# Differential attention beside a delta rule: second probabilities scaled by VectorE, diagonal blocks of inverses loaded to their places

## The chip, the core and the metric

The kernel runs on one core of one Trainium2 chip. The metric is the device time of one launch in microseconds (us). The engines are TensorE (PE, and PEld for its weight loads), VectorE (DVE), ScalarE (ACT), GpSimd (POOL), and SyncE (SP), whose queue issues the transfers here.

## The reference, cut to what matters

Two transformer blocks follow each other. The change lies in the mixer of the first, which has two halves that run at the same time: differential attention (four heads) and a gated delta rule (GDN; two directions, ten tiles of 128 tokens, four heads).

```python
def diff_attn(q, k, v, lam):          # 8 query blocks of 128, 4 heads, 1280 keys
    s = einsum('bqhid,bkhid->bhiqk', qi, k)
    p = softmax(s, axis=-1)
    a = p[:, :, 0] - lam * p[:, :, 1]
    return einsum('bhqk,bkhe->bqhe', a, v)
...
def gdn_chunked(q, k, v, g, beta, s0, need_out):
    a_mat = eye + bc * (kc @ kc.T) * dec_strict       # unit lower triangular
    sol = triangular_solve(a_mat, [bc * exp(Gc) * kc, bc * vc])
    def step(s, xs):
        u = ub_n - w_n @ s
        o = qd_n @ s + aqk_n @ u
        return gl_n * s + kd_n.T @ u, o
```

## The kernel before

`stage_mixer` first projects and prepares (`gdn_prep` writes the triangular matrices of every tile to `Ad` in DRAM; `gdn_invert` inverts the four 32x32 diagonal blocks of each matrix on VectorE and writes the inverses and their transposes to `XT` in DRAM). Then comes the stretch in which both halves run side by side; it is called the mixing stage below.

- **Attention.** A unit (`da_unit`) is one block of 128 queries of one head; there are 32. Per softmax `i` (two of them) and per piece of 512, 512 and 256 keys: two matmuls make a score piece `sc` in PSUM (three such buffers), VectorE reduces its minimum (L707, tile `dst`), ScalarE takes the exponential into `E` (L708), which frees the PSUM buffer. Six tiny VectorE operations (L712 to L719) give a factor per row and piece. Then the second probabilities are scaled by GpSimd (L722: three `tensor_mul` per unit, in place on `E[1]`), and VectorE joins both (L723, `scalar_tensor_tensor`). Ten transposes on TensorE (L729), copies by ScalarE (L730), ten products with the values, and a norm whose power is taken by GpSimd (L93) end the unit.
- **Head switch.** `da_load` loads queries, keys and values of a head and splits them into a high and a low part: queries' low parts on VectorE (L674, tile `da_ql`), keys' low parts (L677, tile `da_ka`) on VectorE for head 0 and on GpSimd for heads 1 to 3, two operations per head.
- **Delta rule.** `gdn_merge` builds the whole 128x128 inverse of a tile pair (one tile per direction) from the diagonal blocks: it loads the blocks into `mc` (L489, one transfer per direction, 128 partitions), copies them by sixteen VectorE copies of 32x4x32 into the block diagonals of `X` (L496, tile `mX`, two buffers per direction) and `T` (L497, tile `mT`, one buffer per direction), and fills the off-diagonal blocks by small matmuls. `gdn_step` then uses `X` (first product of the step, `ga<-sv,mX`) and updates the state.
- **What sets the order.** The program emits one delta step per four units from the fourth step on (`DAU`, `DA0`); a scheduler then lays out every engine's instructions, so each engine runs a fixed order, and SP's queue too: a transfer that waits for its buffer holds all that stand behind it.

```python
    for d, t in enumerate(ts):
        c = wk.tile([128, 8, 32], F32, name=f"mc{d}", bufs=2)
        nc.sync.dma_start(c, K.XT[d, t].rearrange("x h b j i -> (b j) (x h) i"))
```

Of the kernel before, what the change touches and what calls it, by code (L numbers as in the profile page):

```python
# [10 lines left out]
F32 = mybir.dt.float32  # L11
# [5 lines left out]
ALU = mybir.AluOpType  # L17
# [452 lines left out]
def gdn_merge(K, wk, ts, first):  # L470
# [3 lines left out]
    nc = K.nc  # L474

    def new(name, n=128, bufs=2):
        return wk.tile([128, 4, n], F32, name=name, bufs=bufs)

    def bank():
        return K.ga.tile([128, 4, 128], F32, name="gm", bufs=GMB)  # L480

    B = [new(f"mB{d}", bufs=1) for d in range(2)]
    X, T = [K.X[d][len(K.done) % 2] for d in range(2)], K.T
    K.done.append(ts)
    k = [new(f"mk{d}") for d in range(2)]
    Xc, Tc = [], []
    for d, t in enumerate(ts):
        c = wk.tile([128, 8, 32], F32, name=f"mc{d}", bufs=2)
        nc.sync.dma_start(c, K.XT[d, t].rearrange("x h b j i -> (b j) (x h) i"))  # L489
        Xc.append(c[:, 0:4])  # L490
        Tc.append(c[:, 4:8])
        nc.sync.dma_start(B[d], K.Ad[d, t].rearrange("h j i -> j h i"))
        nc.sync.dma_start(k[d], K.ktk[t])
        for b in range(4):
            q = slice(b * 32, (b + 1) * 32)
            nc.vector.tensor_copy(X[d][q, :, q], Xc[d][q])  # L496
            nc.vector.tensor_copy(T[d][q, :, q], Tc[d][q])  # L497
    G = new("mG", 64)
    pg = bank()
    pairs = []  # L500
# [3 lines left out]
            pairs.append((d, lo, hi) if d == 0 else (d, hi, lo))  # L504
    for d, F, S in pairs:
        for h in range(4):
            K.mm(pg[S, h, 0:32], B[d][F, h, S], Tc[d][F, h], True, True)
    nc.scalar.activation(G[:, :, 0:32], pg[:, :, 0:32], AF.Copy, scale=-1.0)
    px = bank()
    for d, F, S in pairs:  # L510
        for h in range(4):
            K.mm(px[F, h, 0:32], G[S, h, 0:32], Xc[d][S, h], True, True)
    for d, F, S in pairs:
        nc.scalar.activation(X[d][F, :, S], px[F, :, 0:32], AF.Copy)
    py = bank()
    for d, F, S in pairs:
        for h in range(4):
            K.mm(py[S, h, 0:32], Xc[d][S, h], G[S, h, 0:32], True, True)
    for d, F, S in pairs:
        nc.vector.tensor_copy(T[d][S, :, F], py[S, :, 0:32])  # L520
    pg = bank()
# [136 lines left out]
def da_load(K, hd, lp, h):  # L658
    nc = K.nc
    q = lp.tile([128, L], F32, name="dalq")  # L660
# [4 lines left out]
    nc.sync.dma_start(v, K.vd[:, h * 128:(h + 1) * 128].rearrange("(t p) e -> p t e", p=128))  # L665
    lo, hi = slice(0, 64), slice(64, 128)
    Q, KA = [], []
    sub = (nc.gpsimd if h else nc.vector).tensor_sub
    for i, (a, b) in enumerate(((lo, hi), (hi, lo))):
        qh = hd.tile([128, L], F32R, name=f"da_qh{i}")  # L670
        ql = hd.tile([128, L], F32R, name=f"da_ql{i}")
# [18 lines left out]
def da_unit(K, wk, ek, ps, hd, qb, o):  # L690


    nc = K.nc
# [4 lines left out]
    mn, ls, sc, l2 = (st[:, i] for i in range(4))  # L698
    t = wk.tile([128, 4, 2], F32, name="dsu")
# [87 lines left out]
def stage_mixer(K, cst, dr):  # L787

    nc, I, tc = K.nc, K.I, K.tc
# [21 lines left out]
    with ExitStack() as s0:  # L811
# [4 lines left out]
        with ExitStack() as s1:  # L816
# [6 lines left out]
            with ExitStack() as s2:  # L823
                wk = K.pool(s2, "cvw", 2)
# [30 lines left out]
            wk = dp  # L855
# [14 lines left out]
        with ExitStack() as s1:  # L870
# [40 lines left out]
            n, u = 0, da()  # L911
# [1607 lines left out]
```

## Time and profile before

| | |
|---|---|
| median of three runs | 3204.37 us (3204.27 to 3206.47) |
| the profiled execution's own time | 3200.96 us |
| its span (first to last instruction) | 3199.2 us |
| share of the span busy: PE / DVE / ACT / POOL | 91% / 75% / 51% / 21% |
| mixing stage in the span | about 545 to 1015 us |

The profiled execution ran 3.4 us below the median; its span leaves out 1.8 us around the first and last instruction. The busy shares are averages over stages of different limits, so the mixing stage is read by itself below. PE's busy time is the union of the times of matmuls that overlap; it is an upper bound of the work.

### The profile page before, as it was taken

Reading aid. Unit: us, or ns where it says so; the run is one execution under the profiler, and the core shown is the slowest. Engines: PE = TensorE matmul, PEld = TensorE weight load, DVE = VectorE, ACT = ScalarE, POOL = GpSimd, SP = SyncE. Lnnn points to the kernel's source line nnn. Section 1 sums busy time; section 2 is a strip of 40 time slices with the busy share of each in tenths; the row PEclk is TensorE's granted clock in tenths of the full one; section 3 lists DMA queues with packets and bytes.
Section 4 is the critical chain, followed back from the end, with each engine's and each line's share of the span. In section 5 each row is a group of like instructions: output and inputs, shape, how many; then the busy total and the mean of one; then the engine's idle time right before and its main releaser. Section 6 shows DMA issues by size and latency. Waiting matters only on the chain.

```text
span 3199.2 us, 45340 instructions
## 1 busy us (share of the span) xinstructions
PE 2898.8 (91%) x15797; PEld 2389.5 (75%) x15797; DVE 2396.0 (75%) x4935; ACT 1634.3 (51%) x3127; POOL 661.9 (21%) x606
## 2 busy tenths in 40 slices
PE   6899998779898969999998799998798999999999
PEld 3677886768786748888776677777677788888787
DVE  4388676897887599999988599986556686555675
ACT  3333454464675238877776577654443243333343
POOL 1000111244555511112001334432125000000000
PEclk8999998789899979999999899999899999999999
DMA  6366565443325469999996223224565323333833
GB/s 219 109 212 194 178 189 185 128 140 111 89 89 181 146 227 379 393 393 375 374 372 222 69 66 93 69 71 129 156 220 192 111 77 107 110 109 99 293 112 102
DMA packets 366211, 567.04 MB, mean 177 GB/s; under 512 B 72581, under 2 KB 207646, under 8 KB 365982
## 3 DMA queue, kind: packets, MB, share of 16 engines
q1 hardware_dynamic: 361374, 547.37, 50.5%
q0 software_dynamic: 4608, 16.78, 2.1%
q8 instruction: 124, 2.03, 0.3%
q14 instruction: 105, 0.86, 0.1%
HBM read 446.12 MB, written 117.95 MB: 176 GB/s over the span
## 4 chain that ended last, share of the span: by engine, by line
PE 65%; DVE 18%; DMA 7%; issue 4%; ACT 3%; POOL 2%; SPq 1%; DVEq 0%; ACTq 0%; POOLq 0%
PE pj L57 38%; PE py L57 5%; PE pu L57 5%; PE pg L57 5%; PE ga L57 2%; PE lg L57 2%; DVE dst L707 2%; DMA s5wo<-s5o 1%; DVE E L723 1%; DVE bjv L1778 1%; DMA wmod<-in_w_mod_dram 1%; PE sc L57 1%; PE tp L1252 1%; PE gm L57 1%; DVE tw L1101 1%
## 5 line engine op out<-in xcount | busy, mean ns | idle before, releaser
L1229 DVE TENSOR_TENSOR wl<-wraw,wh 128x1024 fp32r<-128x1024 f32 x384 | 446.6, 1219 | 10.7 <-ACT wh L1228 10.4
L1228 ACT ACTIVATE wh<-wraw 128x1024 fp32r<-128x1024 f32 x384 | 391.8, 1060 | 77.7 <-PE pu L57 39.7
L57 PE MATMUL pj<-hh,wh 128*128 128x512 f32 (+1 forms) x768 | 297.7, 388 | 14.4 <-ACT uo L1928 9.5
L57 PE MATMUL pj<-hl,wh 128*128 128x512 f32 (+1 forms) x768 | 293.3, 382 | 0.0
L57 PE MATMUL pj<-hh,wl 128*128 128x512 f32 (+1 forms) x768 | 292.4, 382 | 0.0
L57 PEld LDWEIGHTS pj<-hh,wh 128*128 128x128 f32 x768 | 146.1, 190 | 46.5 <-ACT uo L1928 12.6
L57 PE MATMUL pj<-wh,hh 128*128 128x512 f32 (+1 forms) x400 | 160.8, 403 | 16.9 <-DVE g L2018 9.0
L57 PEld LDWEIGHTS pj<-hh,wl 128*128 128x128 f32 x768 | 145.4, 190 | 30.4 <-issue 3.7
L57 PEld LDWEIGHTS pj<-hl,wh 128*128 128x128 f32 x768 | 145.8, 190 | 27.1 <-issue 2.9
L708 ACT ACTIVATE E<-sc,dst 128x512 f32<-128x512 f32 (+1 forms) x192 | 117.4, 616 | 94.4 <-DVE dst L707 84.1
L57 PE MATMUL pj<-wh,hl 128*128 128x512 f32 (+1 forms) x400 | 158.9, 399 | 1.7 <-DVE hl L214 1.5
L57 PE MATMUL pj<-wl,hh 128*128 128x512 f32 (+1 forms) x400 | 160.2, 401 | 0.0
L75 ACT ACTIVATE wh<-wraw 128x1024 fp32r<-128x1024 f32 (+2 forms) x88 | 88.7, 1014 | 91.9 <-DMA wraw<-in_w_in_dram 37.3
L76 POOL TENSOR_TENSOR wl<-wraw,wh 128x1024 fp32r<-128x1024 f32 (+1 forms) x44 | 100.7, 2293 | 140.2 <-ACT wh L75 139.9
L57 PE MATMUL sc<-da_ka,da_qh 128*128 128x512 f32 (+1 forms) x192 | 83.6, 438 | 35.7 <-ACT E L708 32.0
L1292 POOL DMA_INDIRECT xacc<-ye,ix x16 | 49.9, 3121 | 318.7 <-DVE ye L1291 238.0
L707 DVE TENSOR_REDUCE dst<-sc 128x1 f32<-128x512 f32 (+1 forms) x192 | 108.6, 593 | 8.2 <-PE sc L57 7.2
L57 PE MATMUL pu<-wl,xh 128*128 128x512 f32 x256 | 101.3, 396 | 9.4 <-DVE wl L1229 9.2
L722 POOL TENSOR_TENSOR E<-E,dst 128x512 f32<-128x512 f32 (+1 forms) x96 | 95.7, 1024 | 55.8 <-DVE dst L719 27.2
L1775 ACT ACTIVATE bja<-isc,bca 128x384 bf16<-128x384 f32 (+2 forms) x96 | 79.4, 827 | 51.3 <-DVE bca L1793 25.4
L57 PEld LDWEIGHTS pj<-wh,hh 128*128 128x128 f32 x400 | 77.7, 195 | 34.8 <-DVE g L2018 9.4
L57 PE MATMUL pg<-wl,xh 128*128 128x512 f32 x256 | 102.8, 402 | 0.5 <-DVE wl L1229 0.5
(825 smaller groups left out, 8508.8 us busy)
## 6 DMA issues: line engine op xcount, KB each, us to landing
wraw<-in_w_gate_dram SPq DMA_DIRECT2D x64, 1024.0 KB
wraw<-in_w_up_dram SPq DMA_DIRECT2D x64, 1024.0 KB
wraw<-in_w_down_dram SPq DMA_DIRECT2D x64, 1024.0 KB
wraw<-in_w_in_dram SPq DMA_DIRECT2D x52, 512.0 KB
raw<-hsd SPq DMA_DIRECT2D x38, 512.0 KB
mw<-in_w_mod_dram SPq DMA_DIRECT2D x32, 512.0 KB
raw<-in_w_ffn_gate_dram SPq DMA_DIRECT2D x22, 512.0 KB
raw<-in_w_ffn_up_dram SPq DMA_DIRECT2D x22, 512.0 KB
```

The costliest lines, as they stand in the source:

```text
L57: self.nc.tensor.matmul(out, lhsT, rhs, start=start, stop=stop, skip_group_check=True)
L75: nc.scalar.activation(h, raw, AF.Copy)
L76: self.sub(l, raw, h.bitcast(F32))
L707: nc.vector.tensor_reduce(mn[:, i, j:j + 1], p[:, :n], axis=AX.X, op=ALU.min)
L708: nc.scalar.activation(e[:, c0:c0 + n], p[:, :n], AF.Exp, bias=mn[:, i, j:j + 1], scale=-1.0, accum_out=ls[:, i, j:j + 1])
L722: nc.gpsimd.tensor_mul(e1, e1, sc[:, 1, j:j + 1].to_broadcast([128, n]))
L723: nc.vector.scalar_tensor_tensor(e0, e0, sc[:, 0, j:j + 1], e1, op0=ALU.mult, op1=ALU.add)
L1101: self.V.tensor_tensor(b[:, :, i], a[:, :, 0], a[:, :, 1], op=ops[i])
L1228: nc.scalar.activation(h, raw[:, k], AF.Copy)
L1229: nc.vector.tensor_sub(l, raw[:, k], h.bitcast(F32))
L1292: nc.gpsimd.indirect_dma_start(out=K.xacc, out_offset=bass.IndirectOffsetOnAxis(ap=idx[e][:, :1], axis=0), in_=ye, in_offset=None, compute ...
L1775: self.K.nc.scalar.activation(jk[:, :self.n], self.x, AF.Sign, bias=cand, scale=-1.0, accum_out=cnt)
```

## The change

1. The second probabilities are scaled on VectorE (`tensor_scalar` with one scalar per partition) and no longer on GpSimd (`tensor_mul` with a broadcast factor).
2. The keys' low parts of heads 1 to 3 are subtracted on VectorE too.
3. `gdn_merge` loads each diagonal block straight to its place: eight transfers of 32 partitions x 4 x 32 elements (16 KB) per direction, four for `X` and four for `T`, take the place of one transfer of 128 KB and eight copies. The tile `mc` is gone; `T` gets a second buffer per direction, cleared once like the others. The small matmuls read the blocks out of `X` and `T`.

```diff
-    X, T = [K.X[d][len(K.done) % 2] for d in range(2)], K.T
+    X, T = ([Y[d][len(K.done) % 2] for d in range(2)] for Y in (K.X, K.T))
...
     for d, t in enumerate(ts):
-        c = wk.tile([128, 8, 32], F32, name=f"mc{d}", bufs=2)
-        nc.sync.dma_start(c, K.XT[d, t].rearrange("x h b j i -> (b j) (x h) i"))
-        Xc.append(c[:, 0:4])
-        Tc.append(c[:, 4:8])
+        for b in range(4):
+            q = slice(b * 32, (b + 1) * 32)
+            nc.sync.dma_start(X[d][q, :, q], K.XT[d, t, 0, :, b].rearrange("h j i -> j h i"))
+            nc.sync.dma_start(T[d][q, :, q], K.XT[d, t, 1, :, b].rearrange("h j i -> j h i"))
         nc.sync.dma_start(B[d], K.Ad[d, t].rearrange("h j i -> j h i"))
         nc.sync.dma_start(k[d], K.ktk[t])
-        for b in range(4):
-            q = slice(b * 32, (b + 1) * 32)
-            nc.vector.tensor_copy(X[d][q, :, q], Xc[d][q])
-            nc.vector.tensor_copy(T[d][q, :, q], Tc[d][q])
...
-            K.mm(pg[S, h, 0:32], B[d][F, h, S], Tc[d][F, h], True, True)
+            K.mm(pg[S, h, 0:32], B[d][F, h, S], T[d][F, h, F], True, True)
...
-    sub = (nc.gpsimd if h else nc.vector).tensor_sub
+    sub = nc.vector.tensor_sub
...
-        nc.gpsimd.tensor_mul(e1, e1, sc[:, 1, j:j + 1].to_broadcast([128, n]))
+        nc.vector.tensor_scalar(e1, e1, sc[:, 1, j:j + 1], None, op0=ALU.mult)
         nc.vector.scalar_tensor_tensor(e0, e0, sc[:, 0, j:j + 1], e1, op0=ALU.mult, op1=ALU.add)
...
-            K.T = [gk.tile([128, 4, 128], F32, name=f"mT{d}") for d in range(2)]
+            K.T = [[gk.tile([128, 4, 128], F32, name=f"mT{d}{i}") for i in range(2)] for d in range(2)]
```

The scheduler lays the stage out anew; outside it the orders stay, but for two neighbouring loads late on SP. In the changed kernel line numbers behind the merge are 5 lower (L723 is L718 there).

**SP's queue where the mixing stage begins.** Behind the last rows of `gate_proj` (`sgd`) the queue stood like this; `dalq`, `dalk`, `da_v` are queries, keys and values of head 0, `ia` the loads of the third inversion, `sv`, `sqd`, `saq` loads of the first steps. The rows from the first `sqd` to `da_v`, before:

```order
L559 DMA sqd<-Qd 128x512
L428 DMA Ad<-e_4141 128x4x128
L560 DMA saq<-Qk 128x512
L489 DMA mc_5667<-XT 128x8x32
L489 DMA mc_5679<-XT 128x8x32
L604 DMA gsg<-sgd 128x512
L492 DMA mB_5498<-Ad 128x4x128
L492 DMA mB_5499<-Ad 128x4x128
L446 DMA ia<-Ad 16x32x32 x4
L662 DMA dalq<-qrd 128x1024
L663 DMA dalk<-krd 128x1280
L665 DMA da_v<-vd 128x10x128
```

and now:

```order
L423 DMA Qk<-e_4134 128x512
L490 DMA mT_5381<-XT 32x4x32
L428 DMA Ad<-e_4141 128x4x128
L489 DMA mX_5377<-XT 32x4x32
L446 DMA ia<-Ad 16x32x32 x3
L657 DMA dalq<-qrd 128x1024
L658 DMA dalk<-krd 128x1280
L660 DMA da_v<-vd 128x10x128
L446 DMA ia<-Ad 16x32x32 x5
L490 DMA mT_5381<-XT 32x4x32
L489 DMA mX_5377<-XT 32x4x32
L490 DMA mT_5381<-XT 32x4x32
```

The loads of head 0 now follow the last store to `Ad` with one block piece and three `ia` loads between; the blocks of the second direction and the loads of the first steps, which stood ahead of them, stand behind.

**VectorE at a head switch.** `da_ql` and `da_ka` are the low parts of the new head. Before, where the blocks of two merges are copied in one place and the `da_ka` operations of that switch are on GpSimd:

```order
L738 SCALAR_TENSOR_TENSOR o_sb<-atp,oss,dagr 128x128
L712 TENSOR_REDUCE dsu<-dst 128x2
L520 COPY mT_5379<-gm 32x4x32 x2
L520 COPY mT_5380<-gm 32x4x32 x2
L707 TENSOR_REDUCE dst<-sc 128x1
L497 COPY mT_5379<-mc_7153 32x4x32 x2
L497 COPY mT_5379<-mc_6603 32x4x32 x2
L497 COPY mT_5380<-mc_7165 32x4x32 x2
L497 COPY mT_5380<-mc_6615 32x4x32 x2
L674 SCALAR_TENSOR_TENSOR da_ql_8589<-dalq,da_qh_8588 64x1024 x2
L707 TENSOR_REDUCE dst<-sc 128x1 x2
L674 SCALAR_TENSOR_TENSOR da_ql_8598<-dalq,da_qh_8597 64x1024 x2
```

and now:

```order
L672 TENSOR_TENSOR da_ka_7346<-dalk,da_ka_7346 64x1280
L669 SCALAR_TENSOR_TENSOR da_ql_7350<-dalq,da_qh_7349 64x1024 x2
L713 TENSOR_TENSOR dsu<-dsu,nlam 128x1
L672 TENSOR_TENSOR da_ka_7355<-dalk,da_ka_7355 64x1280
L92 TENSOR_SCALAR rstd_t<-oss 128x1
L714 TENSOR_TENSOR dst<-dst,dsu 128x6
L702 TENSOR_REDUCE dst<-sc 128x1 x2
L717 TENSOR_SCALAR E_6973<-E_6973,dst 128x512 x2
L717 TENSOR_SCALAR E_6973<-E_6973,dst 128x256
L733 SCALAR_TENSOR_TENSOR o_sb<-atp,oss,dagr 128x128
L707 TENSOR_REDUCE dsu<-dst 128x2
L718 SCALAR_TENSOR_TENSOR E_6957<-E_6957,dst,E_6973 128x512 x2
```

The copies out of `mc` are gone, the subtractions and the three scalings of each unit (L717) stand in VectorE's own order. Over the whole kernel VectorE loses 160 copies and gains 96 scalings and 6 subtractions, POOL loses those 102 (and gains two clears), and SP gains 140 transfers (160 pieces for 20).

## Rows read from the trace of the kernel before

**Rows 1.** Busy time in stretches: from:to, length, PE, PEld, DVE, ACT, POOL, clock, DMA share
```profile
545.00:580.00 35.00, 18.23 (x235) 15.80 (x234) 24.45 (x66) 14.70 (x40) 9.03 (x9) 0.61 1.05 274
...
580.00:680.00 100.00, 87.57 (x832) 77.92 (x832) 94.54 (x233) 52.49 (x147) 39.16 (x40) 0.86 0.34 101
680.00:705.00 25.00, 13.33 (x125) 11.24 (x122) 23.31 (x47) 13.73 (x30) 13.36 (x9) 0.69 0.59 173
...
sum 435.00, PE 371.28 PEld 325.80 DVE 381.42 ACT 258.37 POOL 215.34; mean PE 92.82 PEld 81.45 DVE 95.36 ACT 64.59 POOL 53.84
...
760.00:800.00 40.00, 39.20 (x477) 36.01 (x476) 31.06 (x72) 21.31 (x70) 20.45 (x20) 1.00 0.38 113
```

**Rows 2.** Waits from 580 to 1010 us: waiter, awaited, us in total, times, longest
```profile
ACT E L708 <- DVE dst L707: 84.1, 55, 7.0
```

**Rows 3.** VectorE by line and shape, 580 to 1015 us: busy us, mean ns, idle before
```profile
L723 DVE SCALAR_TENSOR_TENSOR E<-E,dst,E 128x512 f32<-128x512 f32 x64 | 68.5, 1084 | 8.0 <-POOL E L722 7.8
...
L496 DVE COPY mX<-mc 32x128 f32<-32x128 f32 x56 | 22.2, 396 | 7.6 <-PE ga L57 4.0 <-PE gm L57 2.9
L674 DVE SCALAR_TENSOR_TENSOR da_ql<-dalq,da_qh 64x1024 fp32r<-64x1024 f32 x13 | 21.3, 1640 | 0.2
L497 DVE COPY mT<-mc 32x128 f32<-32x128 f32 x60 | 20.0, 334 | 2.5 <-DMA mc<-XT 1.8
L723 DVE SCALAR_TENSOR_TENSOR E<-E,dst,E 128x256 f32<-128x256 f32 x32 | 18.8, 589 | 0.1
...
L715 DVE TENSOR_TENSOR dst<-dst 128x6 f32<-128x6 f32 x32 | 10.8, 336 | 4.1 <-ACT dst L714 3.8
```

**Rows 4.** GpSimd by line in the same stretch, the two lines that move
```profile
L722 POOL TENSOR_TENSOR E<-E,dst 128x512 f32<-128x512 f32 (+1 forms) x96 | 95.7, 1024 | 55.8 <-DVE dst L719 27.2 <-ACT E L708 21.3 <-DVE rstd_t L92 6.2
...
L677 POOL TENSOR_TENSOR da_ka<-dalk,da_ka 64x1280 fp32r<-64x1280 f32 x6 | 17.8, 2975 | 3.3 <-PE sc L57 1.7 <-DMA yda<-dy 0.9 <-POOL E L722 0.5
```

**Rows 5.** First head switch in order of time, VectorE, then GpSimd: start us, us
```profile
679.54 2.82 DVE L496 COPY mX<-mc 32x128 f32<-32x128 f32 x1
...
679.40 2.88 POOL L677 TENSOR_TENSOR da_ka<-dalk,da_ka 64x1280 fp32r<-64x1280 f32 x1 [0.91 <-DMA yda<-dy]
```

**Rows 6.** Undisturbed prices, VectorE: groups (busy us, mean ns), then single lines (ns min/median/max)
```profile
L166 DVE TENSOR_SCALAR x<-x,ss 128x1024 f32<-128x1024 f32 x10 | 7.5, 753 | 6.1 <-POOL ss L93 6.1
L212 DVE TENSOR_SCALAR xT<-xT,modS,md 128x512 f32<-128x512 f32 x16 | 7.5, 542 | 0.1
...
L212 DVE TENSOR_SCALAR xT<-xT,modS,md 128x256 f32<-128x256 f32 x8 | 2.7, 412 | 0.0
...
L427 DVE TENSOR_TENSOR e<-e,kks 128x512 f32<-128x512 f32 x20 | 13.8, 688 | 7.8 <-ACT e L426 7.7
...
L677 DVE TENSOR_TENSOR da_ka<-dalk,da_ka x2: 1484/1486/1487, 583.0 to 586.1; 64x1280 fp32r<-64x1280 f32 x2
...
L674 DVE SCALAR_TENSOR_TENSOR da_ql<-dalq,da_qh x16: 1217/1222/3843, 575.2 to 838.5; 64x1024 fp32r<-64x1024 f32 x16
...
L715 DVE TENSOR_TENSOR dst<-dst x32: 149/165/1416, 597.4 to 1006.8; 128x6 f32<-128x6 f32 x32
...
L496 DVE COPY mX<-mc x80: 204/218/2829, 548.3 to 881.2; 32x128 f32<-32x128 f32 x80
```

**Rows 7.** SP's queue: issue of the block loads, a wait, the queries of head 0
```profile
L489 SPq DMA_DIRECT2D mc<-XT x20: 370/432/957, 544.7 to 799.6; - x20
...
SPq L559 <- PE ga L57: 67.6, 11, 13.6
...
568.58 0.48 SPq L662 DMA_DIRECT2D dalq<-qrd  x1
```

**Rows 8.** A landing of `mc` in the chain; the products that open the delta steps
```profile
736.47 3.11 DMA mc<-XT
...
L57 PE MATMUL ga<-sv,mX x160: 270/275/582, 566.1 to 968.4; 128*128 128x128 f32 x160
```

More of the change, by code (lines that the diff above doesn't have):

```diff
@@ L482, in gdn_merge @@
     B = [new(f"mB{d}", bufs=1) for d in range(2)]
-    X, T = [K.X[d][len(K.done) % 2] for d in range(2)], K.T
+    X, T = ([Y[d][len(K.done) % 2] for d in range(2)] for Y in (K.X, K.T))
     K.done.append(ts)
     k = [new(f"mk{d}") for d in range(2)]
-    Xc, Tc = [], []
     for d, t in enumerate(ts):
-        c = wk.tile([128, 8, 32], F32, name=f"mc{d}", bufs=2)
-        nc.sync.dma_start(c, K.XT[d, t].rearrange("x h b j i -> (b j) (x h) i"))
-        Xc.append(c[:, 0:4])
-        Tc.append(c[:, 4:8])
+        for b in range(4):
+            q = slice(b * 32, (b + 1) * 32)
+            nc.sync.dma_start(X[d][q, :, q], K.XT[d, t, 0, :, b].rearrange("h j i -> j h i"))
+            nc.sync.dma_start(T[d][q, :, q], K.XT[d, t, 1, :, b].rearrange("h j i -> j h i"))
         nc.sync.dma_start(B[d], K.Ad[d, t].rearrange("h j i -> j h i"))
         nc.sync.dma_start(k[d], K.ktk[t])
-        for b in range(4):
-            q = slice(b * 32, (b + 1) * 32)
-            nc.vector.tensor_copy(X[d][q, :, q], Xc[d][q])
-            nc.vector.tensor_copy(T[d][q, :, q], Tc[d][q])
     G = new("mG", 64)
@@ L511, in gdn_merge @@
         for h in range(4):
-            K.mm(px[F, h, 0:32], G[S, h, 0:32], Xc[d][S, h], True, True)
+            K.mm(px[F, h, 0:32], G[S, h, 0:32], X[d][S, h, S], True, True)
     for d, F, S in pairs:
@@ L517, in gdn_merge @@
         for h in range(4):
-            K.mm(py[S, h, 0:32], Xc[d][S, h], G[S, h, 0:32], True, True)
+            K.mm(py[S, h, 0:32], X[d][S, h, S], G[S, h, 0:32], True, True)
     for d, F, S in pairs:
@@ L880, in stage_mixer @@
             K.X = [[gk.tile([128, 4, 128], F32, name=f"mX{d}{i}") for i in range(2)] for d in range(2)]
-            K.T = [gk.tile([128, 4, 128], F32, name=f"mT{d}") for d in range(2)]
-            for t in (*K.X[0], *K.X[1], *K.T):
+            K.T = [[gk.tile([128, 4, 128], F32, name=f"mT{d}{i}") for i in range(2)] for d in range(2)]
+            for t in chain(*K.X, *K.T):
                 nc.gpsimd.memset(t, 0.0)
```

## The prediction

> **What bounds the kernel now.** I read the table of slices first, then the busy times by stretch, the waits, the groups by line and shape, and last the order of time at one place. All parts of the change act between 545 and about 1015 us, where attention and the delta rule share the engines; what follows is shifted by whatever this stretch gives or takes. From 580 to 1015 us VectorE is busy for 381.4 of 435 us (88%), PE for 371.3 (85%, matmuls that overlap, so less work than that), ScalarE for 258.4 (59%), GpSimd for 215.3 (49%) [rows 1]. VectorE is the nearest to a bound: ScalarE stands 84.1 us waiting for VectorE's minima, its longest wait of the stretch [rows 2], and until its exponential is done the score buffer isn't free for PE. PE alone can do more: from 760 to 800 us, with VectorE at 31.1 of 40 us, it is busy for 39.2 [rows 1].
>
> VectorE's own times are not its work. A copy of 32x128 takes 218 ns at the median, but 396 and 334 ns in the mean of the stretch and 2829 at worst [rows 3, 6]. The order of time says why: the copy that begins at 679.54 us, just behind the start of GpSimd's subtraction of the keys, takes 2.82 us and ends with it [rows 5]. In that place PE falls to 13.3 of 25 us [rows 1]. So what leaves GpSimd makes VectorE quicker.
>
> **The change part by part, in VectorE's time from 580 to 1015 us.**
>
> 1. Copies of blocks removed: 22.2 + 20.0 = 42.2 us [rows 3].
> 2. Keys' low parts added: 6 x 1.486 = 8.9 us, the price they have for head 0 [rows 6]. On GpSimd they cost 17.8 us [rows 4].
> 3. Scalings added: 64 of 128x512, 32 of 128x256. The trace has the operation with two scalars per partition at 542 and 412 ns, which makes 64 x 0.542 + 32 x 0.412 = 47.9 us, the upper end. With one scalar it is there at 128x1024 only, 753 ns; the slope between the two others is 0.508 ns an element, so that 512 elements come to 493 ns and 256 to 363: 43.2 us, the lower end [rows 6]. I take 43, the same form of operation.
> 4. The joining operations behind them (L723) get quicker. The 64 long ones take 1084 ns, an undisturbed operation with two inputs of that size 688 ns [rows 3, 6]: 25.3 us lie in the disturbance. Between nothing and all of it I take 20, since the scaling beside which they run leaves GpSimd (95.7 of its 215.3 us [rows 4]), and other work stays there. The 32 short ones get nothing.
> 5. Queries' low parts at a switch: 13 x (1.640 - 1.222) = 5.4 us [rows 3, 6]; I take 5, the subtraction beside them being gone.
> 6. Tiny operations: L715 alone loses 32 x (336 - 165) ns = 5.5 us [rows 3, 6]. I put the other small lines, inversions among them, at as much again, 11 in all (an estimate from that row), and take 5, since GpSimd's work falls from 215.3 to 101.8 us; ends 0 and 11.
> 7. The scalings are themselves disturbed by what stays on GpSimd. The copies paid about 0.15 us each (365 against 218 ns) with GpSimd busy for 49%; with 23% left that is 0.07 x 96 = 7 us more.
>
> The sum is -42.2 + 8.9 + 43 - 20 - 5 - 5 + 7 = **-13 us**; with the ends of 3 to 6 it lies between +16 (no relief at all) and -26.
>
> On term 7 a page of the Trainium skill is weighed. The copy of 2.82 us ended with GpSimd's 2.88 us [rows 5]. The page "SBUF — State Buffer", section "SBUF: two separate sides", says that VectorE and GpSimd share one pair of ports under an exclusive lock, and that the loser waits for the other's whole instruction. The two times agree with that. By that rule a scaling that begins inside a remaining GpSimd operation waits for half of its roughly 1.1 us in the mean, 96 x 0.23 x 0.55 = 12 us instead of 7 (an estimate from the page's rule), and the sum would be -8.
>
> **Waits.** Today a unit's scaling is a detour over GpSimd: three operations of 1.02 us in the mean, about 3.1 us, and VectorE's join waits 7.8 us in all for them [rows 3, 4]. Now VectorE does them in 1.35 us and waits for nobody; the rest of the unit starts sooner, and GpSimd's powers and delta products no longer queue behind the scalings. I take the 7.8 us, give the shorter chain nothing more, and call it **-7**. Late next is VectorE itself, whose minima now stand behind three more operations of a unit.
>
> **Start of the stage.** From 545 to 580 us transfers are at their limit (DMA share 1.05), PE is idle for half of the time [rows 1], and head 0's queries are issued only at 568.58 us [rows 7], behind the delta rule's loads. Now they stand directly behind the last stores to `Ad`, and VectorE, which makes what those stores carry, no longer has some 40 copies in between (of 160 in all, 116 lie behind 580 us [rows 3]). I expect the first scores about 10 us sooner. The first delta step, at 566.1 us before [rows 8], comes later by more than that, and part of its work now lies beside attention instead of in idle time. Bounds: 0 (all given back) and -12; I take **-8**.
>
> **SP's queue.** 160 pieces for 20 loads: at 0.43 us of issue (370 at the least [rows 7]) that is 60 us more of issuing in 470. Nothing is hidden by bytes, which stay the same; the queue has room, as it stands 67.6 us waiting for one kind of load alone [rows 7]. A merge's pieces can go as soon as the step two before has used the buffer. Steps are (968.3 - 566.1)/9 = 45 us apart [rows 8], the issue of 16 pieces takes 6.9 us, a landing 3.1 us [rows 8], so that they are there about 35 us before they are needed. I cost them at nothing; the cover is that one step of lead. `T`'s second buffer adds two clears on GpSimd ahead of the stage and no wait.
>
> The Trainium skill speaks against this part. The same page, section "Door 1: The DMA port swizzle", says that a transfer into 32 partitions reaches 8 of 16 ports, with 189 against 328 GB/s at 1 MiB. For the 2.6 MB of all blocks that would be 14 us instead of 8 (an estimate from the page), spread over ten merges; as long as the lead holds, the sum stays as it is. No row before shows a load of this shape.
>
> Sum: -13 - 7 - 8 = **-28 us**. The profiled execution took 3200.96 us (span 3199.2), so it would take 3173; the median of the runs, 3.4 us above it, goes from 3204.4 to **3176 us**.
>
> **Rivals.** What a measurement can tell from no change is about 0.2%, 6.4 us.
>
> - *PE fills the room.* If VectorE was what kept PE idle, PE reaches everywhere the 98% that it has from 760 to 800 us: 371.3/0.98 = 379 instead of 435 us, -56, so 3148. For it: that row. Against it: the DVE sum falls by 13, not by 56. 0.15.
> - *The relief is not there.* If VectorE's operations stay stretched, because delta products and powers on GpSimd hit them as before, terms 4 to 6 vanish: -42.2 + 8.9 + 43 + 7 = +17, against -7 and -8 elsewhere: 3206, no change. For it: VectorE's bare work grows (160 copies at 0.218 are 35 us, additions 52). Against it: the copy that ended with GpSimd's subtraction [rows 5]. 0.13.
> - *Blocks come late: slower.* A piece needs the buffer itself, where the old load filled a spare tile. If a merge's 16 pieces are issued only when PE is at it (because SP is held by an earlier load that waits for the steps), each of nine merges costs 6.9 + 3.1 = 10 us, with all engines' orders fixed behind it: +90 - 28 = +62, 3266. It decides once SP stands more than one step (45 us) behind. For it: those 67.6 us in which the queue is held. Against it: no single wait there is over 13.6 us [rows 7]. 0.08. The skill's page, section "The DMA setup-cost knee", gives about 2 us to every transfer; were they paid one after another, a merge's pieces would take 32 us (an estimate from the page), still inside the step.
>
> **How the numbers follow.** My forecast, -14 to -45 us (3159 to 3190), has 0.55. A smaller gain, -2 to -14, because half of the relief falls into waits on PE, has 0.09. With the rivals that makes 1. Faster by over 0.2%: 0.55 + 0.15 + 0.07 = 0.77; within it, 0.02 of the small gain and 0.11 of the second rival, 0.13; slower, 0.08 and 0.02 of the second, 0.10. The range goes from the first rival's time, 3148, to 3202, short of the second: some 0.06 is left out below and 0.14 above.
>
> **What would show it.** Right: scalings near 0.5 us, L723's long form at 0.75 us or below, GpSimd at about 100 us in the stage, first scores ahead of 580 us, and PE above 88% in it. Wrong: L723 still at 1 us; PE waiting for transfers of blocks (`mX`, `mT`) by more than 3 us a merge; VectorE's busy time unchanged with ScalarE's wait for its minima above 84 us; or a stage as long as before with VectorE well below 88%, which would say that another chain sets it.

## The result and the profile after

The change makes the kernel 1.3% faster. The median goes from 3204.57 us (3204.27 to 3206.47, four runs) to 3160.99 us (3155.63 to 3164.55, four runs). The ratio is 0.9867, with a 95% interval of 0.9853 to 0.9881, or -43.6 us where -28 was forecast. The profiled execution took 3159.23 us, its span 3157.5 us.

In the changed kernel the lines of attention stand five lower: L702 is the minimum (before L707), L717 the scaling (L722), L718 the join (L723), L669 and L672 the low parts (L674, L677).

To compare the mixing stage I cut it at its own events in each profile, from the first score matmul to the end of the last join. The first fence is the kernel before, by stretch: from:to, length, busy us and count of PE, PEld, DVE, ACT, POOL, then clock, DMA share and GB/s.

```profile
545.00:584.60 39.60, 19.52 (x266) 16.96 (x264) 27.91 (x69) 17.12 (x41) 9.03 (x9) 0.60 1.02 270
584.60:1013.80 429.20, 369.08 (x3244) 323.98 (x3245) 377.80 (x875) 255.33 (x776) 215.34 (x220) 0.91 0.34 102
```

The same cut in the changed kernel, and below it the stretches that answer to [rows 1]:

```profile
545.00:575.70 30.70, 5.83 (x81) 4.55 (x80) 15.16 (x18) 13.71 (x31) 3.58 (x4) 0.59 0.92 212
575.70:974.80 399.10, 362.62 (x3443) 320.48 (x3442) 357.20 (x867) 259.63 (x789) 109.89 (x123) 0.94 0.41 122
580.00:680.00 100.00, 91.13 (x901) 78.99 (x900) 95.58 (x238) 59.05 (x167) 24.50 (x23) 0.89 0.43 125
680.00:705.00 25.00, 23.22 (x280) 21.72 (x280) 18.57 (x46) 10.20 (x33) 6.82 (x7) 1.00 0.66 179
```

The first scores come 8.9 us sooner (575.7 against 584.6), the stage is 30.1 us shorter (399.1 against 429.2), and all that follows moves by what is left, 2.7 us of 41.7 in the span. VectorE's busy time falls by 20.6 us and the rest of the stage, VectorE's idle time, from 51.4 to 41.9 us. PE has 199 more matmuls in the stage, delta work that ran ahead of it before (x266 against x81 in the stretch before the scores), and is busy for 91% of it, before 86%. The last row above lies between two head switches of the changed kernel, so it can't be compared with the 13.3 us of [rows 1]. From the first ScalarE cast of the new head's queries on (675.86 us before, 664.81 now), 25 us show the switch itself, first before, then now:

```profile
675.80:700.80 25.00, 14.01 (x159) 12.70 (x158) 23.40 (x49) 13.73 (x27) 11.47 (x8) 0.77 0.75 210
664.80:689.80 25.00, 20.45 (x209) 17.88 (x208) 23.76 (x44) 17.57 (x41) 6.03 (x6) 0.86 0.62 166
```

PE is busy for 20.4 us there, where it was 14.0.

VectorE by line and shape in that stage, busy us and mean ns; these answer to [rows 3]:

```profile
L718 DVE SCALAR_TENSOR_TENSOR E<-E,dst,E 128x512 f32<-128x512 f32 x64 | 52.9, 851 | 0.0
L717 DVE TENSOR_SCALAR E<-E,dst 128x512 f32<-128x512 f32 x64 | 33.4, 562 | 0.5
L718 DVE SCALAR_TENSOR_TENSOR E<-E,dst,E 128x256 f32<-128x256 f32 x32 | 19.5, 611 | 0.0
L669 DVE SCALAR_TENSOR_TENSOR da_ql<-dalq,da_qh 64x1024 fp32r<-64x1024 f32 x12 | 15.3, 1279 | 4.8 <-ACT da_qh L668 4.7
...
L717 DVE TENSOR_SCALAR E<-E,dst 128x256 f32<-128x256 f32 x32 | 11.1, 346 | 0.0
...
L672 DVE TENSOR_TENSOR da_ka<-dalk,da_ka 64x1280 fp32r<-64x1280 f32 x6 | 9.6, 1606 | 0.2
...
L710 DVE TENSOR_TENSOR dst<-dst 128x6 f32<-128x6 f32 x32 | 6.9, 217 | 4.1 <-ACT dst L709 4.1
```

The copies are gone, the long joins went from 1084 to 851 ns, the queries' low parts to 1279. ScalarE's wait for the minima, 84.1 us in [rows 2], is 56.2:

```profile
ACT E L703 <- DVE dst L702: 56.2, 48, 4.1
...
PE sc L57 <- ACT E L703: 14.5, 14, 3.2
```

The chain of work that ended last, followed through the stage, first before, then now (share of the stage by line; the view ends each row where it ends here):

```profile
by line: DVE dst L707 11.3%; DVE E L723 9.6%; PE ga L57 8.6%; PE sc L57 6.2%; ACT E L708 5.0%; PE gm L57 4.4%; PE atp L57 4.3%; issue 4.1%; DVE mT L497 3.9%; DVE mX L496 3.5%; DVE da_ql L674 3.4%; PE atp L729 2.9%; DVE ia L456 2.5%; POOL E 
by line: PE ga L57 15.0%; PE sc L57 10.6%; PE atp L57 10.4%; DVE dst L702 7.7%; DVE E L718 7.6%; PE gm L57 7.2%; PE atp L724 5.1%; DVE E L717 4.7%; issue 3.2%; DVE ia L456 2.8%; ACT E L703 2.5%; DVE ix L458 2.3%; DVE da_ql L669 2.0%; DMA wr
```

Added up over all its pieces, the chain before ran on VectorE for 216 us, on PE for 117 and on GpSimd for 21.6 (9.9 of them the scalings); now it runs on PE for 196, on VectorE for 137 and on GpSimd for 1.1. The copies (L497 and L496) held 7.4% of it, 32 us.

On SP the queries of head 0 are issued at 559.95 us (568.58 in [rows 7]); a block piece costs what a whole load had cost, 430 ns of issue at the median:

```profile
L489 SPq DMA_DIRECT2D mX<-XT x80: 302/430/1481, 545.9 to 848.8; - x80
```

### The profile page after: what moved, and what is told of

Its sections match the earlier page's. It is cut to its first block, busy times and chain, and to the rows that moved or that the text cites. A ratio compares the mean times of both kernels' runs of the same rounds, so it can differ in the third digit from the quotient of the medians.

```text
span 3157.5 us, 45308 instructions
## 1 busy us (share of the span) xinstructions
PE 2878.8 (91%) x15797; PEld 2373.8 (75%) x15797; DVE 2365.8 (75%) x4877; ACT 1635.1 (52%) x3127; POOL 553.2 (18%) x506
## 4 chain that ended last, share of the span: by engine, by line
PE 67%; DVE 17%; DMA 8%; ACT 3%; issue 3%; SPq 1%; POOL 1%; DVEq 0%; ACTq 0%; POOLq 0%
PE pj L57 39%; PE pu L57 5%; PE pg L57 5%; PE py L57 4%; PE ga L57 3%; PE lg L57 2%; DVE wl L1224 1%; DVE bjv L1773 1%; PE sc L57 1%; PE atp L57 1%; DMA s5wo<-s5o 1%; PE gm L57 1%; DVE dst L702 1%; DVE E L718 1%; DMA wmod<-in_w_mod_dram 1%
## 5 line engine op out<-in xcount | busy, mean ns | idle before, releaser
L57 PE MATMUL pj<-hh,wh 128*128 128x512 f32 (+1 forms) x768 | 296.7, 387 | 10.7 <-ACT uo L1923 7.7
L57 PEld LDWEIGHTS pj<-hh,wh 128*128 128x128 f32 x768 | 145.3, 189 | 42.4 <-ACT uo L1923 10.9
L57 PE MATMUL pj<-wh,hh 128*128 128x512 f32 (+1 forms) x400 | 160.0, 401 | 15.8 <-DVE g L2013 8.1
L703 ACT ACTIVATE E<-sc,dst 128x512 f32<-128x512 f32 (+1 forms) x192 | 117.6, 618 | 57.2 <-DVE dst L702 56.2
L702 DVE TENSOR_REDUCE dst<-sc 128x1 f32<-128x512 f32 (+1 forms) x192 | 109.5, 594 | 10.2 <-PE sc L57 9.2
L1770 ACT ACTIVATE bja<-isc,bca 128x384 bf16<-128x384 f32 (+2 forms) x96 | 79.3, 826 | 51.4 <-DVE bca L1788 24.5
L57 PE MATMUL py<-wh,hl 128*128 128x512 f32 x256 | 98.7, 390 | 2.1 <-DVE hl L66 2.1
L57 PE MATMUL py<-wl,hh 128*128 128x512 f32 x256 | 100.1, 395 | 0.3 <-DVE wl L1224 0.3
```

What stands on the lines that cost most here:

```text
L57: self.nc.tensor.matmul(out, lhsT, rhs, start=start, stop=stop, skip_group_check=True)
L702: nc.vector.tensor_reduce(mn[:, i, j:j + 1], p[:, :n], axis=AX.X, op=ALU.min)
L703: nc.scalar.activation(e[:, c0:c0 + n], p[:, :n], AF.Exp, bias=mn[:, i, j:j + 1], scale=-1.0, accum_out=ls[:, i, j:j + 1])
L1770: self.K.nc.scalar.activation(jk[:, :self.n], self.x, AF.Sign, bias=cand, scale=-1.0, accum_out=cnt)
```

## The experiments

All are whole kernels, each compared with the kernel before, run beside it (medians 3204.6, 3203.5 and 3202.7 us in three groups); each profile is one execution. The first six are the change's three parts alone and in pairs: S the scalings, K the keys' low parts, B the block loads. "Ends" is the end of the stage in the span, and "idle" the stage less VectorE's busy time in it. Each ratio's interval is about 0.0015 to either side, or 5 us.

| kernel | us (against before) | ratio, 95% | stage | ends | VectorE busy | idle |
|---|---|---|---|---|---|---|
| before | 3204.6 | | 429.2 | 1013.8 | 377.8 | 51.4 |
| S | 3192.4 (-12.2) | 0.9960 [0.9948, 0.9973] | 412.4 | 998.6 | 379.2 | 33.2 |
| K | 3189.1 (-15.5) | 0.9956 [0.9940, 0.9973] | 414.0 | 998.0 | 365.1 | 48.9 |
| B | 3193.9 (-10.7) | 0.9965 [0.9952, 0.9977] | 428.2 | 1001.9 | 352.8 | 75.4 |
| S and K | 3183.7 (-19.8) | 0.9939 [0.9922, 0.9956] | 407.4 | 992.8 | 375.7 | 31.7 |
| S and B | 3175.5 (-27.2) | 0.9917 [0.9900, 0.9935] | 404.1 | 978.6 | 360.8 | 43.3 |
| B and K | 3173.1 (-31.5) | 0.9904 [0.9887, 0.9920] | 405.5 | 976.4 | 344.8 | 60.7 |
| all: the change | 3161.0 (-43.6) | 0.9867 [0.9853, 0.9881] | 399.1 | 974.8 | 357.2 | 41.9 |
| all, scaling on ScalarE | 3162.1 (-41.4) | 0.9870 [0.9853, 0.9886] | 392.6 | 966.6 | 319.8 | 72.8 |
| all, one of three on ScalarE | 3161.4 (-41.3) | 0.9878 [0.9860, 0.9897] | 393.0 | 966.7 | 346.3 | 46.7 |
| all, one `T` | 3164.3 (-39.2) | 0.9873 [0.9856, 0.9889] | 402.1 | 975.6 | 351.2 | 50.9 |
| all, detour of the factors | 3169.5 (-33.2) | 0.9902 [0.9885, 0.9920] | 404.3 | 976.3 | 356.8 | 47.5 |
| all, free GpSimd work | 3192.3 (-11.3) | 0.9961 [0.9947, 0.9975] | 433.1 | 1006.7 | 383.8 | 49.3 |
| all, GpSimd work in the unit | 3233.5 (+30.8) | 1.0095 [1.0077, 1.0113] | 456.5 | 1030.0 | 407.9 | 48.6 |

What lies behind the stage takes 2185.4 us before and 2182.7 in the changed kernel, whose orders are the same there, but 2186 to 2197 in the others and 2202 in the last. No edit touches that part, yet the scheduler laid it out otherwise: compared place by place from 1014.4 us on in the changed kernel, VectorE's order differs at 3 of 3133 places before and in "free GpSimd work", at 159 to 276 in the others, and at 1229 in the last. A single execution adds its own scatter (that of "free GpSimd work" lies 7 us above its median), and that the order alone makes the difference is not shown. But a difference between two totals can hold some 10 us that do not come from the stage; the column "ends" is free of them, though it too is one execution of each kernel.

### The scalings alone (S)

```diff
-        nc.gpsimd.tensor_mul(e1, e1, sc[:, 1, j:j + 1].to_broadcast([128, n]))
+        nc.vector.tensor_scalar(e1, e1, sc[:, 1, j:j + 1], None, op0=ALU.mult)
```

> The kernel before with the scalings alone moved to VectorE. Theory A (VectorE's own time sets the stage, priced term by term): scalings +43 to +47 us, joining operations -16 to -20, tiny ones -3, waits for GpSimd -7: +13 to +21 us, so 3217 to 3226. Rival B (the detour over GpSimd was the long way of a unit, and its disturbance of VectorE the main cost): faster by 15 to 30 us, 3175 to 3190. Rival C (all parts hide behind each other): within 6 us of before.

Measured: 3192.39 us (3187.57 to 3194.42, six runs), faster. The stage, and VectorE's lines in it:

```profile
586.20:998.60 412.40, 359.49 (x3250) 315.65 (x3250) 379.19 (x971) 254.78 (x777) 121.22 (x124) 0.93 0.36 106
```

```profile
L723 DVE SCALAR_TENSOR_TENSOR E<-E,dst,E 128x512 f32<-128x512 f32 x64 | 48.4, 779 | 0.1
L722 DVE TENSOR_SCALAR E<-E,dst 128x512 f32<-128x512 f32 x64 | 35.0, 583 | 0.6
...
L497 DVE COPY mT<-mc 32x128 f32<-32x128 f32 x60 | 17.7, 298 | 3.5 <-DMA mc<-XT 2.4 <-PE gm L57 0.5
```

VectorE does 96 operations more and is busy for 1.4 us more: 50.4 us of scalings (35.0 and 15.4) came, the long joins gave 20.1 us back (68.5 to 48.4), the copies 8.7, short operations the rest. Idle time falls by 18.2 us, where the one wait that the profile before named for it was 7.8. Theory A falls. Rival B has the direction, and its range (to 3190) is missed by 2.4 us; the stage ends 15.2 us sooner. That the idle time falls by more than the named wait fits a longer way over GpSimd, but VectorE also has 50.4 us more of its own work to fill waits with.

### The keys' low parts alone (K)

```diff
-    sub = (nc.gpsimd if h else nc.vector).tensor_sub
+    sub = nc.vector.tensor_sub
```

> The kernel before with the keys' low parts of heads 1 to 3 alone moved to VectorE. Theory A: +9 us of subtractions, -5 for the queries' low parts, and the copies of blocks that stood still beside six subtractions of 2.9 us get back 10 to 15 us: -6 to -11 us, 3193 to 3199. Rival (such standstills fall into idle time): 0 to +9 us, 3204 to 3214.

Measured: 3189.14 us (3186.03 to 3191.10, four runs).

```profile
584.00:998.00 414.00, 365.81 (x3237) 323.87 (x3238) 365.12 (x881) 255.48 (x776) 197.52 (x214) 0.91 0.35 106
```

VectorE takes on six subtractions and is busy for 12.7 us less. The copies of blocks fall from 396 and 334 ns to 296 and 262, about 10 us of it. So the long operation of [rows 5] hurt all that stood beside it, more than theory A had given it.

### The block loads alone (B)

The edit is part 3 of the change, whole, with the two lines above left as they were.

> The changed kernel with the scalings and the keys' low parts put back on GpSimd, so the block loads alone. Theory A: -42 us of copies and -9 us for the earlier first scores, most of it on the path: 3154 to 3170, as fast as the whole change. Rival B (GpSimd's work is what costs): -9 us for the start and little else, 3188 to 3196. Rival D (blocks come late): slower than before, above 3211.

Measured: 3193.92 us (3190.19 to 3200.16, six runs). The stage, VectorE's joins, and a wait:

```profile
573.70:1001.90 428.20, 373.94 (x3446) 328.86 (x3446) 352.84 (x767) 259.94 (x791) 223.85 (x226) 0.91 0.38 113
```

```profile
L718 DVE SCALAR_TENSOR_TENSOR E<-E,dst,E 128x512 f32<-128x512 f32 x64 | 73.4, 1160 | 13.5 <-POOL E L717 13.4
...
L718 DVE SCALAR_TENSOR_TENSOR E<-E,dst,E 128x256 f32<-128x256 f32 x32 | 25.9, 810 | 0.1
```

```profile
POOL E L717 <- DVE dst L714: 44.3, 18, 6.9
```

The scores begin at 573.7 us, 10.9 sooner, and the stage is as long as before, with 202 more matmuls in it. Of the copies' 42.2 us VectorE's busy time keeps 25.0: the joins take 12.0 us more, beside the same GpSimd. And even those 25 turn into idle time (51.4 to 75.4). Theory A falls by 24 us and more; B, with a stage that stays at its length, holds. Which chain holds that stage is not shown: no wait of the list is long enough alone, and the chain of this run's profile can't be followed back into the stage. What the 160 pieces cost beside the 20 loads is not measured by itself either, since every run with the pieces is also without the copies.

### Block loads with the keys (B and K)

The changed kernel with the scalings back on GpSimd (the first diff, reversed).

> The changed kernel with the scalings alone put back on GpSimd (block loads and keys' low parts on VectorE stay). Theory A: it lacks the +13 to +21 us of the scalings, so 3140 to 3150, faster than the whole change. Rival B: the scalings' move carries the gain, so without it 3185 to 3195.

Measured: 3173.06 us (3171.40 to 3174.24, four runs).

```profile
570.90:976.40 405.50, 361.04 (x3446) 320.35 (x3446) 344.84 (x773) 258.93 (x791) 204.35 (x220) 0.95 0.41 120
```

Neither theory: in the total, moving the scalings is worth 12 us here too. In the stage it is worth less: 6.4 us of its length, and 1.6 at its end (976.4 against 974.8); the other 10 us lie behind it, where the order differs. VectorE is busy for 12.4 us less without the move, and idle for 18.8 more (60.7 against 41.9).

### Scalings with the keys (S and K)

The kernel before with both short diffs.

> The kernel before, with the scalings and the keys' low parts on VectorE, and the blocks still copied by VectorE. The two alone gave -12.2 and -15.5 us, blocks alone -10.7, all three -43.6. Theory A (the parts add up, each with its own mechanism): -26 to -33, 3172 to 3179, and first scores at about 585 us, as before. Theory B (VectorE's copies cost path time once both others are on VectorE): little is gained, -5 to -18, 3187 to 3200, and the block loads are then worth 26 to 38 us in the presence of the others, as against 10.7 alone.

Measured: 3183.71 us (3182.89 to 3189.58, four runs), between the two theories.

```profile
585.40:992.80 407.40, 360.63 (x3249) 318.58 (x3249) 375.73 (x977) 256.10 (x776) 101.82 (x118) 0.92 0.36 108
```

S and K overlap: -27.7 apart, -19.8 together. Both take GpSimd's work away from VectorE's side, and a disturbance can be removed only once; that this is the reason is argued and not shown. The block loads then bring 23.8 us more, as against 10.7 alone: 9.7 at the start, 8.3 in the stage, the rest behind it.

### Scalings with the block loads (S and B)

The changed kernel with the second diff reversed. (Heads 1 to 7 in the expectation are heads 1 to 3; there are four.)

> The changed kernel with the keys' low parts of heads 1 to 7 back on GpSimd, so scalings and block loads alone. Scalings alone gave -12.2, blocks alone -10.7; the keys' low parts took a further 7.4 us off the scalings and 20.8 us off the block loads. Theory A (each long operation of GpSimd costs what it stands in the way of VectorE at a head switch): the keys are worth 8 to 20 us here too, 3169 to 3181. Theory B (with 70 us less of other VectorE and GpSimd work the head switch has room): under 6 us, 3161 to 3167.

Measured: 3175.47 us (3173.56 to 3179.80, four runs): theory A by the total, 14.5 us above the changed kernel. In the stage it is 5.0 us of length and 3.8 at its end (978.6 against 974.8), which would fit theory B; the rest lies behind it. The stage, and the line that paid:

```profile
574.50:978.60 404.10, 362.93 (x3443) 319.79 (x3442) 360.78 (x862) 259.53 (x791) 131.55 (x130) 0.95 0.41 120
```

```profile
L669 DVE SCALAR_TENSOR_TENSOR da_ql<-dalq,da_qh 64x1024 fp32r<-64x1024 f32 x12 | 27.0, 2252 | 0.3 <-ACT da_qh L668 0.2
```

Six subtractions on GpSimd make twelve operations of VectorE 0.97 us longer each (2252 against 1279 ns), 11.7 us, and the subtraction itself costs VectorE only 9.6. The stage pays less than half of that.

### Disturbance or detour: GpSimd work that nobody waits for

First without any dependency:

```diff
         nc.vector.tensor_scalar(e1, e1, sc[:, 1, j:j + 1], None, op0=ALU.mult)
+        nc.gpsimd.tensor_mul(K.dum[:, :n], K.dum[:, :n], K.dsc[:, 0:1].to_broadcast([128, n]))
```

> The changed kernel, with one more multiplication on GpSimd per scaling, of the same size, on a scratch tile that nothing else reads: nobody waits for it, but GpSimd is busy about 96 us more in the stage. It leaves the result as it is. It separates the two things that GpSimd's scalings cost: being in the chain of a unit, and disturbing VectorE. Theory A (disturbance, as the prediction's terms 4 to 6 have it): the joining operation's long form goes back from 851 ns towards 1.08 us, VectorE's busy time in the stage rises by 15 to 25 us, and the time by as much: 3175 to 3188. Theory B (the detour: what the change gains comes from the unit's shorter chain): VectorE's operations are stretched as in A, but the time rises by under 7 us: up to 3168.

Measured: 3192.27 us (3189.93 to 3199.42, five runs), 31 us more than the changed kernel. It doesn't answer its question. The scheduler put the 96 free operations together at the front of GpSimd's order:

```profile
L718 POOL TENSOR_TENSOR dum<-dum,dsc x96: 607/1039/2168, 527.0 to 695.6; 128x512 f32<-128x512 f32 x64, 128x256 f32<-128x256 f32 x32
```

There they hold the delta rule's own work on GpSimd, and TensorE waits for them once for 18.2 us; the joins stay at 857 ns. So the second form reads the unit's factors, which puts it where the scalings had been:

```diff
+        nc.gpsimd.tensor_mul(K.dum[:, :n], K.dum[:, :n], sc[:, 1, j:j + 1].to_broadcast([128, n]))
```

> The changed kernel, with one GpSimd multiplication more per scaling, of the same size, on a scratch tile, that reads the unit's own factors: so it stands in GpSimd's order where the kernel before has its scalings, behind the same wait for VectorE, and nobody waits for its result. Against the changed kernel it adds GpSimd's work and its place in the queue, without the detour. Theory A (disturbance and GpSimd's queue): most of what moving the scalings was worth with the other two parts in place (31.5 to 43.6, 12 us) is given back or more, +10 to +30: 3171 to 3191, VectorE's busy time in the stage up by 15 us or more. Theory B (the detour): under 6 us more than the changed kernel, up to 3167, with VectorE's operations stretched beside idle time that absorbs it.

Measured: 3233.52 us (3229.58 to 3236.57, four runs), slower than both kernels. The stage, and VectorE in it:

```profile
573.50:1030.00 456.50, 387.06 (x3444) 339.27 (x3442) 407.88 (x867) 258.01 (x790) 203.44 (x205) 0.90 0.35 103
```

```profile
L702 DVE TENSOR_REDUCE dst<-sc 128x1 f32<-128x512 f32 x128 | 86.0, 683 | 14.7 <-PE sc L57 14.0 <-issue 0.2
L719 DVE SCALAR_TENSOR_TENSOR E<-E,dst,E 128x512 f32<-128x512 f32 x64 | 60.1, 966 | 0.0
L717 DVE TENSOR_SCALAR E<-E,dst 128x512 f32<-128x512 f32 x64 | 55.3, 904 | 0.7
L717 DVE TENSOR_SCALAR E<-E,dst 128x256 f32<-128x256 f32 x32 | 31.7, 989 | 0.0
```

One unit in order of time, VectorE above (all three scalings, then the second and the third by themselves), GpSimd below (start us, us):

```profile
788.15 2.71 DVE L717 TENSOR_SCALAR E<-E,dst 128x512 f32<-128x512 f32 x3
788.55 1.26 DVE L717 TENSOR_SCALAR E<-E,dst 128x512 f32<-128x512 f32 x1
789.74 1.13 DVE L717 TENSOR_SCALAR E<-E,dst 128x256 f32<-128x256 f32 x1
...
788.26 1.28 POOL L718 TENSOR_TENSOR dum<-dum,dst 128x512 f32<-128x512 f32 x1 [0.16 <-DVE dst L714]
789.61 1.10 POOL L718 TENSOR_TENSOR dum<-dum,dst 128x512 f32<-128x512 f32 x1
```

VectorE's busy time rises by 50.7 us, 42.5 of it in the scalings (33.4 + 11.1 to 55.3 + 31.7), and the stage by 57.4; idle time by 6.7. Disturbance it is, and at more than theory A's size: the 96 operations of GpSimd, put beside scalings that VectorE does itself, cost VectorE about half their own time (50.7 of 93.6 us). The short scaling takes longer than the long one, so this is waiting, not work. The minimum, which reads PSUM, stays at 683 ns.

By the page "SBUF — State Buffer" of the Trainium skill, section "SBUF: two separate sides", GpSimd and those VectorE operations that have two SBUF inputs or run in a mode that takes two ports hold one pair of ports in turn, each for a whole instruction. The trace agrees on who is hit: scalings and joins are, the minimum isn't. It agrees on the whole instruction too: the second scaling ends some 0.28 us and the third 0.15 us after the GpSimd operation beside it. Of the 96 scalings of this run 67 take over 0.6 us; each of these ends 0.28 us (the long) or 0.15 us (the short) after the end of an operation of GpSimd.

The total rises by 17 us more than the stage's end moves (72.5 against 55.2). That part lies in the second block, which no edit touches, but whose order differs most in this run.

### The detour by itself

```diff
+    sg = wk.tile([128, 2, 3], F32, name="sg")
+    nc.gpsimd.tensor_copy(sg, sc)
+    sc = sg
     for j, (c0, n) in enumerate(cs):
```

> The changed kernel, with the unit's six factors per partition copied by GpSimd, and the scalings and joins reading that copy: a detour over GpSimd in each of the 32 units, with 32 tiny operations in place of 96 large ones. Theory A (disturbance): nothing to speak of, within 5 us of the changed kernel, 3156 to 3166. Theory B (the detour: a unit waits behind what GpSimd has in its queue, and VectorE, whose order is fixed, waits with it): +8 to +20, 3169 to 3181, with VectorE waiting for GpSimd's copy by 10 us or more in all (it waited 7.8 us for the scalings before).

Measured: 3169.50 us (3165.96 to 3175.29, four runs), at the lower edge of theory B, but not by its mechanism:

```profile
L720 DVE TENSOR_SCALAR E<-E,sg 128x512 f32<-128x512 f32 x64 | 35.1, 590 | 3.1 <-POOL sg L716 3.0
```

VectorE waits 3.0 us in all, where 10 were expected. The stage is 5.2 us longer, but begins sooner and ends only 1.5 us later. Its chain passes through GpSimd's copies for 0.8 us, and once through the landing of a block piece for 6.5:

```profile
688.32 6.54 DMA mX<-XT
```

So a hop of 32 tiny operations costs next to nothing that can be told from other differences. It explains little of the 17 to 32 us of idle time that moving the scalings takes away (51.4 to 33.2, 48.9 to 31.7, 75.4 to 43.3, 60.7 to 41.9). The rest I put down to the three long operations that stood in the detour and to GpSimd's queue behind them: the chain before ran through GpSimd for 21.6 us. No run shows that by itself.

### The cover of the block loads: one buffer of `T`

```diff
-            K.T = [[gk.tile([128, 4, 128], F32, name=f"mT{d}{i}") for i in range(2)] for d in range(2)]
+            K.T = [[gk.tile([128, 4, 128], F32, name=f"mT{d}{i}") for i in range(1)] for d in range(2)]
```

The buffer's number is then taken modulo the number of buffers of its tile.

> The changed kernel, with a single buffer of T for each direction, as the kernel before had it: the pieces of T can then be written only when the step before has read its T, so the lead of a step (45 us) is taken from half of the pieces. Theory A (the lead is what hides the pieces): each of nine merges waits for its 8 pieces of T, issue 3.4 us and landing 3.1 us, and what stands behind them on SP's queue (the queries and keys of the next head among them) comes later too: +15 to +60 us on the changed kernel, 3176 to 3221, with waits for mT of 3 us or more a merge. Theory B (a merge is off the path, attention fills the wait): under 7 us, 3155 to 3168.

Measured: 3164.30 us (3163.22 to 3165.48, four runs), the same as the changed kernel within the interval: theory B. SP does wait for the buffer, and it doesn't show in the time:

```profile
SPq L490 <- PE gm L57: 36.6, 10, 7.1
```

### VectorE relieved further: scalings on ScalarE

All three of a unit, then only the middle one (`if j == 1`, else VectorE):

```diff
-        nc.vector.tensor_scalar(e1, e1, sc[:, 1, j:j + 1], None, op0=ALU.mult)
+        nc.scalar.activation(e1, e1, AF.Copy, scale=sc[:, 1, j:j + 1])
```

> The changed kernel, with the scalings of the second probabilities on ScalarE (an activation with a scale per partition) in place of VectorE. VectorE loses the 64 + 32 scalings that take 33.4 + 11.1 = 44.5 us in the changed kernel's stage of 399 us; ScalarE, busy for 259.6 us there, gains some 64 x 0.59 + 32 x 0.38 = 50 us (the prices of its evictions of the same sizes). Theory A (VectorE's busy time still sets the stage): 25 to 45 us less than the changed kernel, 3116 to 3136. Theory B (PE and the chain of one unit set it, VectorE's 44.5 us lie beside PE's 91%): within 10 us of the changed kernel, 3151 to 3171, PE's busy time in the stage at 362 us as before. Theory C (ScalarE's exponentials stand behind the scalings and PE waits for them): slower than the changed kernel, 3171 to 3195, with PE's wait for ScalarE before a score matmul above the 14.5 us that it has there.

> The changed kernel, with the middle of a unit's three scalings (512 columns) on ScalarE and the two others on VectorE: VectorE loses 32 x 0.56 = 18 us in the stage, ScalarE gains 32 x 0.59 = 19 us. All three on ScalarE left the time as it was (3162.1), with VectorE 37 us shorter and the stage 6.5 us shorter in the profile. Theory A (the two engines' order matters, VectorE and ScalarE should work side by side): -5 to -12, 3149 to 3156. Theory B (PE, at 91% of the stage, sets it, whoever scales): within 5 us of the changed kernel, 3156 to 3166.

Measured: 3162.11 us (3158.77 to 3164.72, four runs) and 3161.41 us (3157.63 to 3168.33, four runs), both as fast as the changed kernel. The stages, all three first:

```profile
574.00:966.60 392.60, 360.05 (x3425) 319.67 (x3423) 319.83 (x771) 305.87 (x884) 107.63 (x123) 0.95 0.42 124
```

```profile
573.70:966.70 393.00, 355.75 (x3419) 314.72 (x3418) 346.27 (x834) 279.70 (x820) 111.71 (x123) 0.96 0.42 123
```

With 37.4 us less on VectorE the stage is 6.5 us shorter; with 10.9 us less it is 6.1 us shorter. VectorE no longer sets it, which the chain through the changed kernel's stage says too. PE is busy for 90 to 92% in all three. Theory B of both holds. The stage even ends 8 us sooner (966.6 and 966.7 against 974.8), but what lies behind it, in another order, takes 6 to 8 us longer, and no version beats the change.

## Why the prediction was right, and where its working was not

The time, 3160.99 us, lies in the range, 15 us below the forecast; that it does is in part luck, as the parts show. Of its three sums the signs hold: VectorE -20.6 (forecast -13), idle time -9.5 (waits -7), start -8.9 (-8). What would show it right came mostly: scalings at 0.56 and 0.35 us, GpSimd at 110 us, scores ahead of 580 us, PE at 91%, and none of the listed waits in the changed kernel's stage names a block piece. The joins, at 851 ns, reached neither 0.75 nor stayed at 1 us. A slip in the sum: the ends that terms 3 to 6 give make +22 and -25 us, not +16 and -26.

- *Terms 2, 3 and 5* held: keys 9.6 us (8.9 forecast), scalings 44.5 (43), queries -4.8 (-5). With term 7 on top the scalings would have been 50, with the 12 us that the prediction works out for the same term 55; neither came.
- *Term 4* was too large: -15.6 for the long joins, not -20, and the short ones paid 0.7. The scalings alone gave 20.1.
- *SP's queue* at nothing fits, but not by the lead: with half of the lead gone the time stayed. *Blocks come late* fell with it.
- The page "SBUF — State Buffer" of the Trainium skill, section "Door 1: The DMA port swizzle", gives a transfer of 1 MiB into 32 partitions 189 GB/s, one into 128 partitions 328. No run here shows those rates for pieces of 16 KB. In the changed kernel the chain passes through the landing of one, ahead of the stage, for less than the 3.11 us of a whole load in [rows 8]:

```profile
545.93 2.46 DMA mX<-XT
```

- *PE fills the room* went part of the way: the stage is 399 us, not 379, and its chain now lies on PE for half of its length.

By parts the working was wrong, and the errors cancelled. Its own terms give the scalings +43 - 20 - 5 + 7 - 7 = +18, the keys +8.9 - 5 = +4, the blocks -42.2 - 8 = -50. Measured alone: -12.2, -15.5 and -10.7, or -15.2, -15.8 and -11.9 at the end of the stage.

Two steps failed. The first is term 1, **the copies priced as time of the path**. A saved microsecond of VectorE is one of the stage only where VectorE would not stand idle instead: B alone took 25.0 us off VectorE and 1.0 off the stage. That the chain before ran through the copies for 32 us didn't help: without them another chain was nearly as long. Part of it is the 202 matmuls that the earlier start moved into the stage, 4.9 us of PE (373.9 against 369.1), which the prediction put into its -8. With the other parts in place (S and K to all) the same edit took 18.5 us off VectorE and 8.3 off the stage. Besides, 10 us of the copies' 42.2 was the disturbance by the keys' subtraction (K alone gives it back), so the price was partly that of another part of the change.

The second is in the waits: **"I take the 7.8 us, give the shorter chain nothing more"**. Moving the scalings took 17 to 32 us of VectorE's idle time in every pair, about twice the join's wait for GpSimd in the kernel that it is moved in (7.8 us before, 9.0 in K, 13.4 in B, 9.3 in B and K). The named wait is only that of the join, while the chain before ran through GpSimd for 21.6 us. That the difference is the next units' minima, exponentials and transposes, which stand behind the join, is argued and not shown. And VectorE's busy time, which the terms let rise by 25 us for S, rose by 1.4, since in S the copies and the small lines were relieved too.

## What to carry to other kernels

Where two engines disturb each other and share a chain, price an edit in the stage and not in the busy time of one engine: an operation that only fills idle time is worth little (B: 25.0 us of VectorE, 1.0 of the stage), and one that is a step in every unit's chain can take about twice the wait it shows out of idle time. Try the parts alone, and compare the stage and not the total, since the scheduler may lay out the rest anew; a right total can hide parts that are wrong by 20 to 40 us each. And try to take work off GpSimd that stands beside VectorE's operations on SBUF, even if VectorE has to do it itself: in S alone 50.4 us of scalings came to VectorE, and 49.0 went from the lines beside them.

## What was not expected

- The short scalings beside GpSimd's work took 989 ns and the long ones 904, against 346 and 562 without it. A delayed one waits for the end of GpSimd's operation, however short it is itself.
- 160 transfers of 16 KB in place of 20 of 128 KB, each with the issue time of a large one (430 ns), showed no cost in the time, with one buffer less either (3164.30 against 3160.99 us).
- PE's granted clock moved with the stage: 0.91 before, 0.94 after, both between its two levels, 1.2 and 2.4 GHz; over the 25 us of the first head switch 0.77 with PE busy for 14.0 us, and 0.86 with 20.4. B had as many matmuls at 0.91 as the change at 0.94, and they took PE 373.9 us against 362.6, a gain that no term held.
